# Output projection weights split twice, first gate and up products in another order, and squares of three norms summed on TensorE

## The chip, the cores and the metric

The kernel runs on one core of a Trainium2 chip. A core has a matrix engine (TensorE, PE in the rows; its weight loads are PEld), a vector engine (VectorE, DVE), an engine for functions of one element (ScalarE, ACT), GpSimd (POOL) and a queue that issues transfers (SyncE, SP). Each works its own list of instructions in order; semaphores tie the lists together. The metric is the time of one execution on the device in microseconds, from the first to the last instruction and the little around them.

## The reference

Two decoder layers work on 1024 tokens of width 1024 in f32. Each layer normalises its input, projects it with one matrix for three token mixers, joins their outputs, projects them back (`w_out`) and adds; then it normalises again, and a feed-forward part of width 2816 with gate, up and down follows. A last norm ends it. Cut to what matters:

```python
def rms_norm(x, g):
    y = x * rsqrt(mean(x * x, axis=-1) + 1e-6)
    return y * g

for l in range(2):
    h = rms_norm(x, attn_norm_g[l])
    pa, pb, pc = split(h @ w_in[l])
    ya, yb, yc = rwkv7(pa), dilated_attention(pb), latent_attention(pc)
    x = x + concat(ya, yb, yc) @ w_out[l]
    h = rms_norm(x, ffn_norm_g[l])
    x = x + (silu(h @ w_gate[l]) * (h @ w_up[l])) @ w_down[l]
return rms_norm(x, final_norm_g)
```

## The kernel before

Activations lie transposed: the model's width on the 128 partitions (8 tiles, `KD`), tokens along the columns, in two halves of 512 (`hf`). To reach f32 accuracy a factor is split into a high part, rounded to a faster format (a cast on ScalarE), and a low part, the difference (`split`, on GpSimd or VectorE). `mm3` makes three matmuls from high times high and the two mixed terms. So each weight tile of 128 x 512 costs a load (`wr`), a cast (`wh`), a subtraction (`wl`) and then feeds 4 times 3 matmuls.

The work is written as many small strands (generators). `Flow.run` keeps a clock of estimates for each engine and always lets the strand go on that could start first, so the order of every queue comes out of its costs, and a change in one strand can shift the others. `loader` feeds the weights: `raws` limits the raw tiles, `ring` the split ones that wait. For keys where `again(k)` is true it splits nothing: the first half of the sequence has written the pair of parts to `pairs_dram`, and the second half reads both back. Before, that holds for the input projection ("in") and the output projection ("wo").

In `ffn`, the output projection runs over 8 output tiles for each half (`wo`), adds the residual (`add_x`), and `normed(hf)` normalises that half. Its result is cast and split (`put`), and sums and differences of the halves are formed (`sums`), because gate and up are multiplied by a scheme of seven products for each 2 x 2 block (`PRODUCTS`, `ORDER`). Products 1 and 2 need no sums. Product 2 goes into the bank of product 1 and so waits until ScalarE has copied that out as `u` (`gather`, `f.read[1]`). For the first `EARLY` = 8 blocks, products 1 and 2 are made ahead of everything else, one block after the other.

A norm (`rstds`) squares each of the 8 tiles on ScalarE, adds the squares on VectorE (`acc`, 7 additions) and has TensorE sum that over the partitions: 4 products with one column for 512 tokens, into a small bank `ssum` (`mean_squares`). Then a square root by iteration follows on VectorE (`rsqrt`, tiles `rh`, `ry`, `rt`) and TensorE spreads it by transposes. `norm1(hf)` does it in front of the input projection, and `last_norm` at the end in three parts of 512, 256 and 256 tokens (`PARTS`) while TensorE still works on the last products of the down projection (`dn`).

Of the kernel before, what the change touches and what calls it, by code (L numbers as in the profile page):

```python
# [10 lines left out]
F32 = mybir.dt.float32  # L11
# [7 lines left out]
L = 2  # L19
T = 1024  # L20
D = 1024
HALF = 512
KD = 8
# [7 lines left out]
EARLY = 8  # L31
# [199 lines left out]
def trunk(ctx: ExitStack, tc: tile.TileContext, xT, pos, vec, con, first, w_in, small, uq, uqr, ukv,  # L231
# [3 lines left out]
    F = Flow()  # L235
# [21 lines left out]
    def mm(out, lhsT, rhs, start, stop, again=False):  # L257

        n, m = cols(rhs), cols(lhsT)
        if lhsT.dtype == F32R:  # L260
            F.op("pe", max(n, 2 * m) * 0.4167 + 3)
        else:
            F.op("pe", 4 * max(n, m) * 0.4167 + 6)
        kw = {"skip_group_check": True} if again else {}
        nc.tensor.matmul(out=out, lhsT=lhsT, rhs=rhs, start=start, stop=stop, **kw)  # L265
# [78 lines left out]
    def few_bank(name):  # L344

        yield Need([few])
        t = yield from bank(name)
        owner[id(t)] = (banks, t, few)
        return t
# [12 lines left out]
    def room(level):  # L362

        return lambda: sum(max(n, 0) for lv, n in reserve.items() if lv < level)
# [74 lines left out]
    def vcol(l, name, i=0):  # L439
        o = l * NVEC + VEC[name] + i  # L440
        return vecs[:, o:o + 1]
# [23 lines left out]
    def split(src, hi, lo, eng):  # L465
# [4 lines left out]
        tt(eng, lo, src, f32(hi), ALU.subtract)  # L470

    raws, ring = Slots(NRAW), Slots(NW)
    pairs_dram = {"in": drp.tile([L, 18, 2, 2, 128, HALF], F32, name="pairs_in"),
                  "wo": drp.tile([L, KD, 2, 2, 128, HALF], F32, name="pairs_wo")}
    at_layer = [0]

    def again(k):
        return k[0] in ("in", "wo") and k[2] == 1

    there = {}  # L480

# [170 lines left out]
            stt(y, t, 1.5, y, ALU.add, ALU.mult)  # L652
        return y

    def mean_squares(xs, where, n, keep, w=HALF):

        acc = None
        mean = cons[:, CON["mean"] + MEANS[n]:CON["mean"] + MEANS[n] + 1]
        squares, ahead = events(len(xs)), Slots(3)

        def square():
            for x, ev in zip(xs, squares):
                x = yield x
                yield Need([ahead])
                sq = yield from page(where, "sq", keep=keep)
                yield "act"
                activation(sq[:, :w], x, ACTF.Square)
                F.set(ev, sq)

        F.spawn(square(), 2)  # L670
        for ev in squares:
            sq = yield ev
            if acc is None:
                acc = sq
            else:
                yield "dve"
                tt("dve", acc[:, :w], acc[:, :w], sq[:, :w], ALU.add)
                free(sq)
                F.give(ahead)
        if squared.t is None:  # L680
            F.set(squared, acc)
        s = yield from few_bank("ssum")
        yield "pe"
        for c in range(w // 128):
            mm(s[:, c:c + 1], acc[:, c * 128:(c + 1) * 128], mean, True, True)
        free(acc)
        return s

    def rstds(xs, where, n, keep=0, w=HALF):

        s = yield from mean_squares(xs, where, n, keep, w)
        y = yield from rsqrt(s[:, 0:w // 128], w // 128, 1e-6, ALU.add)
        yield "pe"
        for c in range(w // 128):
            transpose(s[:, c * 128:(c + 1) * 128], y[:, c:c + 1].to_broadcast([128, 128]))
        return s
# [13 lines left out]
            transpose(s[:, cs_], sq[:, cs_])  # L710
        return s

    def norm(xs, g, out, where, tmp, n=D, keep_x=False, keep=0):

        got, k = [None] * len(xs), ["hx", ("hhi", F32R), ("hlo", F32R)]
        if len(xs) < 3:
            t = yield from pages(where, k * len(xs), keep=keep)
            got = [t[3 * i:3 * i + 3] for i in range(len(xs))]
        r = yield from rstds(xs, tmp, n, keep)
        done = []  # L720

        def one(i, r):
            t, hi, lo = got[i] or (yield from pages(where, k, keep=keep))
            yield "dve"
            stt(t, xs[i].val, g(i), r, ALU.mult, ALU.mult)
            if not keep_x:
                free(xs[i].val)
            done.append(i)
            if len(done) == len(xs):
                free(r)  # L730
            yield from split(t, hi, lo, sub_eng())
            free(t)
            F.set(out[i], (hi, lo))

        for i in range(len(xs)):
            F.spawn(one(i, r), 3)
# [230 lines left out]
    def in_items(l):  # L967
# [5 lines left out]
                    out += units(("in", l, hf, 14), w_in[l, 14])  # L973
        return out

    def out_items(l):
        out = [u for hf in range(2) for c in range(KD) for u in units(("wo", l, hf, c), w_out[l, c])]
        def down(st, s):
            n = (st[1] - st[0]) * 128
            per = HALF // n  # L980
            return [(("d", l, s, c0), [w_down[l, c0 + i, :, st[0] * 128:st[1] * 128] for i in range(per)])
                    for c0 in range(0, KD, per)]

        todo = [(m_, n) for n in range(len(PAIRS)) for m_ in "gu"]

        def blocks(w, a, b, c0=0, n=HALF):

            return [[w[i][:, c0 + o:c0 + o + n]] for i, o in ((a, 0), (b, 0), (b, n), (a, n))]

        mats = {"g": w_gate[l], "u": w_up[l]}  # L990
        for m_, n in todo[:EARLY]:
            a = mats[m_][PAIRS[n][0]]
            out += [((m_, l, n, 1), [a[:, 0:HALF]]), ((m_, l, n, 2), [a[:, HALF:]])]
        for i, (m_, n) in enumerate(todo[:-2]):
            rs = ORDER if i >= EARLY else ORDER[1:3] + ORDER[4:]
            out.append((("S", [(m_, l, n)], rs), [blocks(mats[m_], *PAIRS[n])]))
        out.append((("S", [(m_, l, n) for m_, n in todo[-2:]], ORDER), [blocks(mats[m_], *PAIRS[n]) for m_, n in todo[-2:]]))
        for s in range(NS // KS):
            for c in range(0, KD, 4):
                out.append((("S", [("s", l, s, c), ("s", l, s, c + 2)], ORDER),  # L1000
                            [blocks(w_down[l], i, i + 1, s * 256 * KS, 128 * KS) for i in (c, c + 2)]))
        for s, st in enumerate(STAGES):
            out += down(st, s)
        return out

    def layer(l):
# [14 lines left out]
        def norm1(hf):  # L1021
            xs = x_here if l and hf == 0 else events(KD)
            if xs is not x_here:
                for c in range(KD):
                    F.spawn(load_x(xsrc, c, hf, ["gp"], xs[c], xs_done[c][hf] if l else None, room(1)), 2)
            if hf == 0 and l == 0:
                yield from norm_later(xs)
                return
            yield from norm(xs, lambda i: vcol(l, "g1", i), h[hf], ["gp"], ["gp"], keep=room(1))

        rms = Event()

# [1031 lines left out]
        def ffn():  # L2064
# [126 lines left out]
            def product(key, f, r, B, last=False, n=4):  # L2191
                i, first = BANK[r]
                if first:
                    f.bank[i] = yield from bank(f.name)
                else:
                    yield f.read[{2: 1, 4: 7, 3: 5}[r]]
                p = f.bank[i]
                w = yield W[(*key, r)]
                for k in range(n):
                    b = yield B[r][k]  # L2200
                    s = slice(k * 128, k * 128 + 128)
                    yield "pe"
                    mm3(p, (w[0][:, s], w[1][:, s]), b, first and k == 0, k == n - 1, not first)
                    if last:
                        free(*b)
                drop(w)
                F.set(f.done[r])
# [148 lines left out]
            F.give(raws, 4)  # L2356
            todo = [(m_, n) for n in range(len(PAIRS)) for m_ in "gu"]
            fours = {}
            for m_, n in todo[:EARLY]:
                f = fours[m_, n] = Four("gu")  # L2360
                F.spawn(gather(m_, PAIRS[n], f), 2)
                for r in (1, 2):
                    yield from product((m_, l, n), f, r, Bg)
            for i, (m_, n) in enumerate(todo):
                pair = i >= len(todo) - 2
                if i >= EARLY:
# [120 lines left out]
            if l == L - 1:  # L2487
                def last_norm(hf, c0, c1):
                    xs = xf[hf, c0]
                    r = yield from rstds(xs, where, D, w=c1 - c0)  # L2490
                    for c in range(KD):
                        xt, o = xs[c].val, L * NVEC + c
                        yield "dve"
                        stt(xt, xt, vecs[:, o:o + 1], r[:, 0:c1 - c0], ALU.mult, ALU.mult)
                        yield "dma"
                        dma(outT[c, hf, :, c0:c1], xt, 512 * (c1 - c0))
                        if c1 == HALF:
                            free(xd[c][hf].val)
                    free(r)

                for part in PARTS:
                    F.spawn(last_norm(*part), 2)
# [193 lines left out]
```

## Time and profile before

| | |
|---|---|
| median of 3 runs | 2660.67 us (2658.49 to 2663.81) |
| profiled execution | 2660.13 us, span 2658.3 us |
| TensorE busy | 2553.1 us, 96% of the span |
| VectorE, ScalarE, GpSimd busy | 1720.5, 1127.1, 1121.7 us |
| mean granted TensorE clock | 0.975 |

TensorE's share says that nearly everything lies beside its matmuls. The ends of matmuls are modelled, so a busy TensorE is not TensorE at its peak. Short waits and stretches at half clock are what is left around the work.

### The profile page before, as it was taken

What the parts mean: (1) busy time and instruction counts of PE and PEld (TensorE: products, weight loads), DVE (VectorE), ACT (ScalarE), POOL (GpSimd) and SP (SyncE); (2) the same over time, 40 slices, a digit from 0 to 9 for tenths busy, and PEclk for the clock granted to TensorE, in tenths of its full rate; (3) what the DMA queues carried; (4) which work ended last, traced back from release to release, by engine and by line L of the source; (5) the groups of instructions that cost most, each with busy time, mean ns of one, the idle gap of its engine ahead of it and who ended that gap; (6) DMA issues with size and microseconds to landing.
All of it is one profiled execution on the core that took longest, in us unless ns stands there. A gap on an engine that the chain in (4) does not pass through costs nothing. (4 is left out here: it accounts for less than half of the span.)

```text
span 2658.3 us, 38921 instructions
## 1 busy us (share of the span) xinstructions
PE 2553.1 (96%) x13112; PEld 2045.8 (77%) x13112; DVE 1720.5 (65%) x3410; ACT 1127.1 (42%) x2287; POOL 1121.7 (42%) x882
## 2 busy tenths in 40 slices
PE   7899999999999999999999998999998999999998
PEld 5677865787787888888877787658876888888887
DVE  6856567764778666556567365776448876665556
ACT  6433266662434343322354333766534334333221
POOL 3522132353654444465454122314536444444660
PEclk9899979999999999999999999999999999999999
DMA  7563301139335444796476341101681544349861
GB/s 258 186 235 112 107 22 61 39 131 343 131 134 192 150 171 146 252 351 240 151 256 239 114 170 26 56 27 56 224 313 61 191 170 166 134 141 352 285 205 64
DMA packets 249624, 442.73 MB, mean 167 GB/s; under 512 B 29136, under 2 KB 46800, under 8 KB 249296
## 3 DMA queue, kind: packets, MB, share of 16 engines
q1 hardware_dynamic: 249424, 440.24, 48.2%
q8 instruction: 103, 1.69, 0.3%
q14 instruction: 97, 0.79, 0.1%
HBM read 277.99 MB, written 158.47 MB: 164 GB/s over the span
## 5 line engine op out<-in xcount | busy, mean ns | idle before, releaser
L300 POOL TENSOR_TENSOR wl<-wr,wh 128x512 fp32r<-128x512 f32 (+1 forms) x272 | 400.6, 1484 | 397.0 <-ACT wh L294 301.3
L265 PE MATMUL gu<-hhi,wh 128*128 128x512 f32 x1232 | 483.4, 393 | 20.5 <-ACT u L294 13.3
L265 PE MATMUL gu<-hhi,wl 128*128 128x512 f32 x1232 | 480.5, 391 | 1.1 <-POOL wl L300 1.0
L265 PE MATMUL gu<-hlo,wh 128*128 128x512 f32 x1232 | 481.0, 390 | 0.0
L265 PEld LDWEIGHTS gu<-hhi,wh 128*128 128x128 f32 x1232 | 232.2, 188 | 78.6 <-ACT u L294 16.3
L294 ACT CAST wh<-wr 128x512 fp32r<-128x512 f32 (+1 forms) x392 | 226.1, 591 | 107.4 <-POOL wl L300 31.2
L265 PEld LDWEIGHTS gu<-hhi,wl 128*128 128x128 f32 x1232 | 232.3, 189 | 50.9 <-POOL wl L300 2.0
L265 PEld LDWEIGHTS gu<-hlo,wh 128*128 128x128 f32 x1232 | 232.3, 189 | 47.3
L300 POOL TENSOR_TENSOR wl<-s,wh 128x512 fp32r<-128x512 f32 (+1 forms) x136 | 180.3, 1334 | 192.5 <-ACT wh L294 83.0
L265 PE MATMUL dn<-bhi,wh 128*128 128x512 f32 (+1 forms) x664 | 251.7, 380 | 0.7 <-issue 0.7
L265 PE MATMUL dn<-bhi,wl 128*128 128x512 f32 (+1 forms) x664 | 251.5, 379 | 0.0
L265 PE MATMUL dn<-blo,wh 128*128 128x512 f32 (+1 forms) x664 | 251.5, 379 | 0.0
L265 PE MATMUL inp<-hhi,wh 128*128 128x512 f32 x512 | 217.3, 424 | 13.8 <-ACT wh L294 13.8
L294 ACT CAST wh<-s 128x512 fp32r<-128x512 f32 (+1 forms) x204 | 116.6, 581 | 229.9 <-DVE s L300 189.6
L265 PE MATMUL inp<-hhi,wl 128*128 128x512 f32 x512 | 207.6, 406 | 1.3 <-POOL wl L300 1.3
L265 PE MATMUL inp<-hlo,wh 128*128 128x512 f32 x512 | 207.4, 405 | 0.0
L300 DVE TENSOR_TENSOR x<-x,dn 128x512 f32<-128x512 f32 (+1 forms) x160 | 104.4, 657 | 111.5 <-PE dn L265 82.9
L300 DVE TENSOR_TENSOR v<-u,gu 128x512 f32<-128x512 f32 x132 | 90.0, 682 | 129.2 <-PE gu L265 125.7
L300 POOL TENSOR_TENSOR v<-v 128x512 f32<-128x512 f32 x66 | 97.2, 1476 | 135.6 <-DVE v L300 127.2
L300 POOL TENSOR_TENSOR Hd<-H,pc 128x256 f32<-128x256 f32 x32 | 25.4, 793 | 284.0 <-DVE H L300 254.7
L265 PEld LDWEIGHTS dn<-bhi,wh 128*128 128x128 f32 x664 | 124.9, 188 | 25.4 <-issue 1.5
L265 PEld LDWEIGHTS dn<-bhi,wl 128*128 128x128 f32 x664 | 124.9, 188 | 23.4
(319 smaller groups left out, 5500.0 us busy)
## 6 DMA issues: line engine op xcount, KB each, us to landing
act_dram<-ahi SPq DMA_DIRECT2D x142, 256.0 KB
act_dram<-alo SPq DMA_DIRECT2D x142, 256.0 KB
bhi<-act_dram SPq DMA_DIRECT2D x142, 256.0 KB
blo<-act_dram SPq DMA_DIRECT2D x142, 256.0 KB
wr<-in_w_gate_dram SPq DMA_DIRECT2D x104, 256.0 KB
wr<-in_w_up_dram SPq DMA_DIRECT2D x104, 256.0 KB
wr<-in_w_in_dram SPq DMA_DIRECT2D x72, 256.0 KB
pairs_in<-wh SPq DMA_DIRECT2D x72, 256.0 KB
```

The source lines that it names most:

```text
L265: nc.tensor.matmul(out=out, lhsT=lhsT, rhs=rhs, start=start, stop=stop, **kw)
L294: nc.scalar.copy(out=out, in_=in_)
L300: ENG[eng].tensor_tensor(out=out, in0=a, in1=b, op=op)
```

## The change

It has three edits. First, only the input projection's weights are kept as pairs; the output projection's are loaded and split in both halves. Second, the first products of gate and up are issued in another order: product 2 of a block comes after product 1 of the next block. The weights are asked for in the same order. Third, in three norms (the second half in front of the input projection in both layers, counted as `norm1(1)`, and the last norm) TensorE multiplies each square as it comes and adds up in the bank; VectorE adds nothing.

```diff
-    pairs_dram = {"in": drp.tile([L, 18, 2, 2, 128, HALF], F32, name="pairs_in"),
-                  "wo": drp.tile([L, KD, 2, 2, 128, HALF], F32, name="pairs_wo")}
+    pairs_dram = {"in": drp.tile([L, 18, 2, 2, 128, HALF], F32, name="pairs_in")}
...
-        return k[0] in ("in", "wo") and k[2] == 1
+        return k[0] in pairs_dram and k[2] == 1
...
+        if by_pe:
+            s = yield from few_bank("ssum")
+            for i, ev in enumerate(squares):
+                sq = yield ev
+                yield "pe"
+                for c in range(w // 128):
+                    mm(s[:, c:c + 1], sq[:, c * 128:(c + 1) * 128], mean, i + c == 0, i == len(xs) - 1 and c == w // 128 - 1)
+                free(sq)
+                F.give(ahead)
+            return s
...
+    def early(todo):
+
+        two = [[(*t, r) for t in todo[:EARLY]] for r in (1, 2)]
+        out = [two[0][0]]
+        for i in range(EARLY):
+            out += two[0][i + 1:i + 2] + [two[1][i]]
+        return out
...
-        for m_, n in todo[:EARLY]:
-            a = mats[m_][PAIRS[n][0]]
-            out += [((m_, l, n, 1), [a[:, 0:HALF]]), ((m_, l, n, 2), [a[:, HALF:]])]
+        for m_, n, r in early(todo):
+            out.append(((m_, l, n, r), [mats[m_][PAIRS[n][0]][:, (r - 1) * HALF:r * HALF]]))
...
-            yield from norm(xs, lambda i: vcol(l, "g1", i), h[hf], ["gp"], ["gp"], keep=room(1))
+            yield from norm(xs, lambda i: vcol(l, "g1", i), h[hf], ["gp"], ["gp"], keep=room(1), by_pe=hf == 1)
...
-            for m_, n in todo[:EARLY]:
-                f = fours[m_, n] = Four("gu")
-                F.spawn(gather(m_, PAIRS[n], f), 2)
-                for r in (1, 2):
-                    yield from product((m_, l, n), f, r, Bg)
+            for m_, n, r in early(todo):
+                if r == 1:
+                    fours[m_, n] = Four("gu")
+                    F.spawn(gather(m_, PAIRS[n], fours[m_, n]), 2)
+                yield from product((m_, l, n), fours[m_, n], r, Bg)
...
-                    r = yield from rstds(xs, where, D, w=c1 - c0)
+                    r = yield from rstds(xs, where, D, w=c1 - c0, by_pe=True)
```

How the lists move is shown at three places. The queue of transfers (SP) in layer 0, between the two halves of the output projection; `wh` and `wl` are the pair of weight parts, `pj<-mix_dram` are mixers' outputs for the second half, `park_dram` takes the residual. Before:

```order
L328 DMA wh<-pairs_wo 128x512
L328 DMA wl<-pairs_wo 128x512
L328 DMA pj<-mix_dram 128x512 x3
L328 DMA park_dram<-x 128x512 x3
L328 DMA x<-in_xT_dram 128x512
L328 DMA park_dram<-x 128x512 x5
```

Now:

```order
L328 DMA wr<-in_w_out_dram 128x512 x2
L328 DMA x<-in_xT_dram 128x512
L328 DMA pj<-mix_dram 128x512
L328 DMA park_dram<-x 128x512 x2
L328 DMA wr<-in_w_out_dram 128x512
L328 DMA pj<-mix_dram 128x512 x2
L328 DMA wr<-in_w_out_dram 128x512
L328 DMA pj<-mix_dram 128x512 x2
L328 DMA x<-in_xT_dram 128x512
```

The pair reads are gone, raw weights (`wr`) stand between the rest, and the last loads of the mixers' outputs stand ahead of most of the second half's weights instead of behind the first pair reads.

ScalarE in layer 0 during the first products of gate and up: `u<-gu` copies product 1 of a block out of its bank (the copies shown are those of the fourth and fifth block), `hhi<-hx` casts normed rows, `a<-gu` is silu on a finished pair of products. Before:

```order
L290 ACTIVATE a<-gu 128x512
L294 CAST hhi<-hx 128x512 x3
L294 CAST wh<-wr 128x512
L294 COPY u<-gu 128x512
L294 CAST hhi<-hx 128x512 x2
L294 CAST wh<-wr 128x512
L294 CAST hhi<-hx 128x512 x5
L294 COPY u<-gu 128x512
```

Now (the copy shown is the fifth block's):

```order
L290 ACTIVATE a<-gu 128x512
L294 CAST hhi<-hx 128x512 x3
L294 CAST wh<-wr 128x512
L294 COPY u<-gu 128x512
L294 CAST wh<-wr 128x512
L294 CAST hhi<-hx 128x512 x3
L294 CAST wh<-wr 128x512
```

The fifth copy has moved up: from all blocks' first one on, 19 casts of normed rows stood ahead of it, now 12. On TensorE the matmuls between a block's product 1 and its product 2 were 3 to 35 before, where the order also drew parts of later first products forward; now they are one or two whole products, 12 or 24.

TensorE at the very end, last products of the down projection (`dn`, with the numbers of the buffers) and the third part of the last norm. Before:

```order
L265 MATMUL dn_26168<-bhi_25286,wh_25741 128x256
L265 MATMUL dn_26168<-blo_25287,wh_25741 128x256
L265 MATMUL dn_26168<-bhi_25286,wl_25742 128x256
L265 MATMUL dn_26168<-bhi_25507,wh_25741 128x256
L265 MATMUL dn_26168<-blo_25508,wh_25741 128x256
L265 MATMUL dn_26168<-bhi_25507,wl_25742 128x256
L265 MATMUL ssum_26201<-cons_72,sq_26055 128x1 x2
L275 MATMUL ssum_26201<-cons_72,ry_26204 128x128 x2
```

Now:

```order
L265 MATMUL dn_26258<-blo_25296,wh_25784 128x256
L265 MATMUL dn_26258<-bhi_25295,wl_25785 128x256
L265 MATMUL dn_26258<-bhi_25327,wh_25784 128x256
L265 MATMUL dn_26258<-blo_25328,wh_25784 128x256
L265 MATMUL dn_26258<-bhi_25327,wl_25785 128x256
L265 MATMUL ssum_26079<-cons_72,sq_26266 128x1 x2
L265 MATMUL dn_26258<-bhi_25357,wh_25784 128x256
L265 MATMUL dn_26258<-blo_25358,wh_25784 128x256
L265 MATMUL dn_26258<-bhi_25357,wl_25785 128x256
L265 MATMUL ssum_26079<-cons_72,sq_26277 128x1 x2
L275 MATMUL ssum_26079<-cons_72,ry_26281 128x128 x2
```

The sum over all squares was one row (two products, one for each 128 tokens) after the last matmul; now a row for each square stands between the matmuls, and the last one stays behind them. In the two in-projections the new rows stand in the same way between the `inp` products.

## Rows read from the trace of the kernel before

**Rows 1.** Waits of TensorE: who for whom, us in all, times, longest
```profile
PE ssum L265 <- DVE sq L300: 14.5, 6, 5.1
...
PE gu L265 <- ACT u L294: 13.3, 5, 4.4
...
PE ssum L275 <- DVE ry L309: 10.8, 7, 2.5
```

**Rows 2.** Timeline, TensorE, output projection: start, us, what, [idle before]
```profile
635.00 1.02 PE L265 MATMUL ssum<-cons,sq 128*128 128x1 f32 x8 [2.31 <-DVE sq L300]
...
640.46 1.12 PE L275 MATMUL ssum<-cons,ry 128*128 128x128 f32 x4 [2.50 <-DVE ry L309]
...
1939.19 1.05 PE L265 MATMUL ssum<-cons,sq 128*128 128x1 f32 x8 [2.23 <-DVE sq L300]
```

**Rows 3.** Five stretches with a lowered clock; the first line names the columns
```profile
core 0: us, PE busy (x) PEld busy (x) DVE busy (x) ACT busy (x) POOL busy (x), PEclk, DMA share, GB/s
66.00:77.00 11.00, 8.14 (x24) 6.80 (x25) 10.40 (x20) 2.98 (x6) 5.52 (x5) 0.53 0.51 175
636.00:644.00 8.00, 5.50 (x18) 4.02 (x18) 7.08 (x18) 3.07 (x6) 2.82 (x3) 0.57 1.05 404
720.00:729.00 9.00, 5.80 (x15) 4.55 (x16) 8.96 (x8) 3.06 (x6) 9.00 (x6) 0.62 0.25 86
...
1940.00:1945.00 5.00, 5.00 (x19) 3.96 (x19) 2.86 (x14) 0.62 (x1) 0.85 (x1) 0.66 1.05 402
2015.00:2025.00 10.00, 7.55 (x26) 5.94 (x26) 10.00 (x10) 5.56 (x10) 8.01 (x5) 0.83 0.29 91
```

**Rows 4.** Timeline of ScalarE, and a line group of 590:652 (busy, mean ns)
```profile
635.68 1.91 ACT L294 CAST mhi<-pj 128x512 fp32r<-128x512 f32 x3 [1.55 <-DMA pj<-mix_dram]
...
L300 POOL TENSOR_TENSOR wl<-wr,wh 128x512 fp32r<-128x512 f32 x11 | 14.2, 1299 | 14.1 <-ACT wh L294 5.9 <-DMA pj<-mix_dram 5.9 <-issue 2.2
```

**Rows 5.** Timeline, ScalarE and TensorE, early products of layer 0
```profile
722.57 0.58 ACT L294 COPY u<-gu 128x512 f32<-128x512 f32 x1
...
723.20 0.79 PE L265 MATMUL gu<-hhi,wh 128*128 128x512 f32 x1 [4.40 <-ACT u L294]
```

**Rows 6.** Timeline, TensorE: two matmuls of 512 columns in a row
```profile
740.21 0.39 PE L265 MATMUL gu<-hhi,wh 128*128 128x512 f32 x1
740.43 0.39 PE L265 MATMUL gu<-hlo,wh 128*128 128x512 f32 x1
```

**Rows 7.** Timeline, VectorE: sixth product, low weights and first use, layers 0, 1
```profile
732.07 1.77 DVE L300 TENSOR_TENSOR wl<-s,wh 128x512 fp32r<-128x512 f32 x1
...
743.58 0.69 DVE L300 TENSOR_TENSOR u<-u,gu 128x512 f32<-128x512 f32 x1
...
2036.06 1.75 DVE L300 TENSOR_TENSOR wl<-s,wh 128x512 fp32r<-128x512 f32 x1
...
2047.53 0.69 DVE L300 TENSOR_TENSOR u<-u,gu 128x512 f32<-128x512 f32 x1 [0.18 <-PE gu L265]
```

**Rows 8.** Timeline, weight loads of TensorE (PEld) in the last norm
```profile
2623.38 0.98 PEld L265 LDWEIGHTS ssum<-cons,sq 128*128 128x128 f32 x8
2624.29 0.19 PEld L265 LDWEIGHTS dn<-bhi,wh 128*128 128x128 f32 x1
```

**Rows 9.** Timeline, TensorE: longest waits in the two in-projections
```profile
68.86 1.44 PE L265 MATMUL ssum<-cons,sq 128*128 128x1 f32 x6 [5.10 <-DVE sq L300]
...
1404.41 0.90 PE L275 MATMUL hsum<-cons,sq 128*128 128x128 f32 x3 [4.83 <-DVE sq L313]
```

**Rows 10.** Line group of VectorE from 56 to 69 us
```profile
L300 DVE TENSOR_TENSOR sq<-sq 128x512 f32<-128x512 f32 x7 | 7.6, 1079 | 2.6 <-ACT sq L290 2.6
```

**Rows 11.** The last stage before the end, as one stretch; columns as rows 3
```profile
2600.00:2645.00 45.00, 45.00 (x297) 41.45 (x296) 29.41 (x79) 11.54 (x24) 1.29 (x1) 1.00 0.14 50
```

**Rows 12.** Timeline, VectorE and TensorE: the chain after the last product
```profile
2647.39 0.41 DVE L300 TENSOR_TENSOR sq<-sq 128x256 f32<-128x256 f32 x1
...
2647.95 0.58 PE L265 MATMUL ssum<-cons,sq 128*128 128x1 f32 x4 [2.18 <-DVE sq L300]
```

More of the change, by code (lines that the diff above doesn't have):

```diff
@@ L653, in rsqrt, with mean_squares @@
         return y
-    def mean_squares(xs, where, n, keep, w=HALF):
+    def mean_squares(xs, where, n, keep, w=HALF, by_pe=False):
         acc = None
@@ L687, in mean_squares, with rstds @@
         return s
-    def rstds(xs, where, n, keep=0, w=HALF):
-        s = yield from mean_squares(xs, where, n, keep, w)
+    def rstds(xs, where, n, keep=0, w=HALF, by_pe=False):
+        s = yield from mean_squares(xs, where, n, keep, w, by_pe)
         y = yield from rsqrt(s[:, 0:w // 128], w // 128, 1e-6, ALU.add)
@@ L711, in head_rsqrt, with norm @@
         return s
-    def norm(xs, g, out, where, tmp, n=D, keep_x=False, keep=0):
+    def norm(xs, g, out, where, tmp, n=D, keep_x=False, keep=0, by_pe=False):
         got, k = [None] * len(xs), ["hx", ("hhi", F32R), ("hlo", F32R)]
@@ L718, in norm @@
             got = [t[3 * i:3 * i + 3] for i in range(len(xs))]
-        r = yield from rstds(xs, tmp, n, keep)
+        r = yield from rstds(xs, tmp, n, keep, by_pe=by_pe)
         done = []
```

## Prediction

> **What bounds the kernel now.** I read the waits of TensorE first, then its timeline around the longest of them, then the granted clock beside each, and last the other engines in the same microseconds. The reader is to see that TensorE works nearly all the time, so that added matmuls cost their time in full and only its few waits can be won back. Three of the largest of these waits belong to this change [rows 1]: 14.5 us before the column sums of a norm (ssum), 13.3 us before gate and up's first products, 10.8 us before the transposes that spread a norm's result. Each long wait also lowers the granted clock for some microseconds, to 0.5, which is 1.2 GHz instead of 2.4 [rows 3]. The loss to that is worked out as busy time times what is missing of the clock.
>
> All sums are made against the profiled execution, 2660.13 us (span 2658.3). The median of the three runs is 0.5 us above it.
>
> **Output projection's weights.** At the end of the first half of the sequence, layer 0, TensorE waits 2.31 us for the last square and 2.50 us for the square root; in layer 1 it waits 2.23 us for the square [rows 2]. The clock then costs 5.50 x 0.43 = 2.4 and 5.00 x 0.34 = 1.7 us [rows 3]. That is 11.1 us in all. Why does it have nothing else to do? The second half's matmuls need the mixers' outputs, and the first of these is cast at 635.68, when its load lands [rows 4]. The queue order shows why it is late: the last three of these loads stand behind pair writes and pair reads. The DMA share is then 1.05 [rows 3], so the transfers are the limit. The change takes away, in each layer, 32 writes and 32 reads of 256 KB and adds 16 reads: 12 MB less. The mixers' outputs now stand in the queue before the second half's weights, and 18 matmuls stand between the squares and the transposes instead of 5. So the gap should be filled. The 32 added splits take 1.30 us each on GpSimd [rows 4] and a cast on ScalarE, one for every 12 matmuls; 12 x 0.22 = 2.6 us of TensorE's work covers one [rows 6]. If that cover were gone for the first of a half, a load, cast and subtraction would cost about 2 us. Ends: -11.1 and +2. I take -9, near the measured waits, since the mechanism is seen whole and only some of the wait for the square root may stay.
>
> **First products of gate and up.** The waits of 13.3 us [rows 1] and the clock, 5.80 x 0.38 = 2.2 and 7.55 x 0.17 = 1.3 us [rows 3], make 16.8 us. The longest wait, 4.40 us, ends when ScalarE has copied u out of the bank [rows 5]. The copy is not slow (0.58 us); it stands behind the casts of the normed rows, which wait for VectorE. In the new order this copy, the fifth, stands behind 12 of these casts instead of 19. But VectorE's own order is nearly unchanged, and the next kind of product (the sixth) needs weights whose low part VectorE ends at 732.07 + 1.77 = 733.84 and at 2036.06 + 1.75 = 2037.81 [rows 7]. Its result is added to u at 743.58 and 2047.53 [rows 7]; less the product's own 2.7 us, it could have been issued without a break from 740.9 and 2044.8. So 7 us in each layer can be won before TensorE stands there instead, 14 in all. Ends: 0 (the wait only moves, and costs the clock there) and -16.8. I take -9, two thirds of what VectorE allows, because a shorter wait at the new place also costs some clock.
>
> **Squares added up by TensorE: the price.** A norm over 8 tiles has 8 groups of four products with one column instead of 1, so 28 more products. In the trace the 8 weight loads of one such group (two for each product in f32) begin at 2623.38 and the next matmul's load at 2624.29 [rows 8]: 0.91 us for a group of four. The columns cost nothing; the loads do. Seven more groups are 6.4 us per norm of 512 columns.
>
> The Trainium skill, TensorE: Matmul & The Clock Gate, section "Step-by-step: what each phase is for", says that TensorE pulls weight loads ahead of the matmuls in flight, so that the next tile's weights load while this one is multiplied. By that rule the groups would be nearly free. Rows 8 show it for the first load of a group at most: the other seven have only one-column products to hide behind.
>
> **The two norms of the in-projection (second half, layers 0 and 1).** In layer 0 TensorE waits 5.10 us for the sum [rows 9], and the clock costs 8.14 x 0.47 = 3.8 us [rows 3]: 8.9 us. VectorE spends 7.6 us on the seven additions there [rows 10], in a stretch where it hardly rests, because GpSimd's work makes each 1.08 us long. These go. TensorE gets 6.4 us of groups, spread between products of the projection, so it fills its wait instead of standing. Balance -2.5, and VectorE's later waiters come some 1.5 us sooner: -4. Ends: +6.4 (nothing returns) and -10. In layer 1 the wait is 4.83 us, for another chain that VectorE delivers late [rows 9]; the additions removed are worth about as much as the groups cost. I take 0, ends +6.4 and -6.
>
> **The last norm.** Here TensorE works 45.00 of 45.00 us at full clock up to the end of the last product [rows 11], so the groups are paid in full. The tokens are normed in three parts: 512, 256 and 256 columns. The first adds seven groups of four (6.4 us), the second seven groups of two (3.2), and of the third's eight groups seven stand before the last matmul of the down projection (3.2, where there was none): 12.8 us. After it, TensorE waits 2.18 us for the last addition [rows 12]; that addition (0.41 us) and one in front of it leave the chain, with their handovers: -1.0. Together +11.8, ends +10 and +13.
>
> **Sum.** -9 - 9 - 4 + 0 + 11.8 = -10.2, and 2660.13 - 10.2 = 2649.9; I say 2650.
>
> **Rivals.**
> A: the weights' two stages give everything back: -11.1 - 16.8 - 4 + 0 + 11.8 = -20, so 2640. For it: the mixers' loads clearly move up, and the output projection's earlier end lets VectorE begin sooner. Against: VectorE is without rest in the early products (8.96 of 9 us [rows 3]).
> B: the wait in the early products only moves to the sixth product's weights: gate and up give 2 instead of 9, the rest as forecast, 2657, no change that can be told. For it: rows 7 and VectorE's unchanged order. Against: 7 us per layer lie between VectorE's end and TensorE's start.
> C, slower: the groups are paid everywhere. In the in-projections they come on top, because what TensorE waits for is other work of VectorE and not the seven additions; then both norms cost 6.4, and -9 - 9 + 12.8 + 11.8 = +6.6, 2667. It decides the sign as soon as the stalls return less than the 24.6 us that all groups cost. For it: the 4.83 us of layer 1 are not a wait for these sums. Against: layer 0's 5.10 us are.
> D: the loads are hidden. The norms then give -8.9 and -4.8, the last one -1.0, and the sum is -32.7, 2627. Rows 8 speak against it. This is the skill's rule above.
>
> **How the numbers follow.** Forecast 0.44 (its own range 2643 to 2656), A 0.22, B 0.17, C 0.13, D 0.04. About 0.2%, 5.3 us, can be told from no change. Faster: 0.39 of the forecast's, 0.21 of A's, 0.05 of B's and D's 0.04, 0.69. Same: 0.05, 0.01, 0.11 and 0.02 of C's, 0.19. Slower: 0.12. The order of all five queues is replanned by the change, which can move any other wait by a few us; the forecast's own range has that in it. The range from 2636 to 2664 leaves out D, most of C and a fifth of A.
>
> **What would show it right or wrong.** Right: no wait of TensorE above 1 us among the output projection's matmuls and full clock there; the waits for ScalarE's u below 5 us in total; 0.9 us between the matmuls on both sides of each new group; the last matmul of the down projection coming 12 to 13 us later after the stage's first one than now. A step is wrong if the mixers' second half is still cast after TensorE has run dry, if the groups cost under 0.3 us, if a wait for a square (ScalarE) shows in front of them, or if the sixth product's weights become the early products' wait of more than 4 us. The whole is wrong if the stages that the change does not name move by more than 5 us together.

## The result, and the profile after

The changed kernel is slower: 2673.3 to 2680.9 us in three runs against 2658.5 to 2663.8 us in four, ratio 1.0059 (95% interval 1.0041 to 1.0077), so about +15.7 us. Measured once more beside 19 runs of the kernel before, the ratio was 1.0055 (1.0033 to 1.0076). The first profiled execution took 3050.5 us at a mean granted clock of 0.775 and is left out of these figures, so the profile shown here comes from the second measurement (2686.1 us, span 2684.0, clock 0.968). It is 10 us above the median of its own runs (2675.9), which matters for layer 1 below.

The stages tell where the time is. A stage runs from its first matmul on TensorE to the first one of the next stage (the last one to its own last matmul), in us; "mixers" is what lies between the input projection's last matmul and the output projection's first.

| stage | before | after | difference |
|---|---|---|---|
| input projection, layer 0 | 334.4 | 345.4 | +11.0 |
| mixers, layer 0 | 239.3 | 234.7 | -4.6 |
| output projection, layer 0 | 102.0 | 94.1 | -7.9 |
| gate and up, layer 0 | 437.0 | 438.4 | +1.4 |
| down, layer 0 | 206.9 | 206.1 | -0.8 |
| input projection, layer 1 | 315.8 | 330.8 | +15.0 |
| mixers, layer 1 | 246.9 | 250.7 | +3.9 |
| output projection, layer 1 | 96.3 | 90.5 | -5.8 |
| gate and up, layer 1 | 439.3 | 441.1 | +1.8 |
| down with the last norm, layer 1 | 219.0 | 231.6 | +12.6 |
| after the last product | 12.6 | 11.9 | -0.7 |

TensorE's waits after, as in [rows 1] (who for whom, us in all, times, longest):

```profile
PE gu L265 <- ACT u L294: 14.6, 4, 6.0
...
PE ssum L275 <- DVE ry L309: 10.0, 5, 3.5
...
PE ssum L265 <- ACT sq L290: 2.1, 2, 1.1
PE ssum L265 <- DVE sq L300: 1.5, 1, 1.5
```

The waits for sums of squares fell from 14.5 to 3.6 us, as they were meant to. The waits for `u` did not fall: 14.6 us instead of 13.3, in fewer and longer pieces.

The output projection before, as one stretch for each layer (columns as in [rows 3]):

```profile
582.70:684.80 102.10, 97.29 (x435) 79.88 (x434) 39.96 (x65) 33.19 (x60) 36.66 (x28) 0.97 0.87 310
1891.20:1987.70 96.50, 93.24 (x407) 76.08 (x406) 35.44 (x59) 28.59 (x50) 35.06 (x26) 0.98 0.90 318
```

And after:

```profile
588.90:683.10 94.20, 94.20 (x429) 78.07 (x428) 44.88 (x65) 39.90 (x72) 57.77 (x44) 1.00 0.60 205
1909.00:1999.70 90.70, 90.70 (x407) 75.23 (x406) 39.78 (x59) 37.02 (x66) 55.48 (x42) 1.00 0.61 207
```

TensorE now works without idle time and at full clock there, and the DMA share is down from 0.87 to 0.60. GpSimd works some 20 us more in each layer (36.66 to 57.77, 35.06 to 55.48) and nobody waits for it.

In layer 0's in-projection the 31 us around the norm read so before:

```profile
54.00:85.00 31.00, 23.44 (x106) 18.29 (x107) 27.61 (x43) 14.78 (x28) 16.25 (x13) 0.78 0.49 170
```

And after:

```profile
54.00:85.00 31.00, 29.73 (x118) 25.93 (x119) 15.29 (x27) 10.94 (x22) 14.76 (x12) 0.50 0.51 178
```

TensorE is busy for 29.73 us instead of 23.44, VectorE for 15.29 instead of 27.61. Both are what the change wanted. But the granted clock is 0.50 over the whole stretch, where it was 0.78. The timeline of TensorE after shows what stands there, in place of the 5.10 us of waiting in [rows 9]:

```profile
55.27 0.80 PE L265 MATMUL inp<-hhi,wh 128*128 128x512 f32 x1 [3.21 <-ACT wh L294]
55.85 1.81 PE L265 MATMUL ssum<-cons,sq 128*128 128x1 f32 x8
57.53 0.77 PE L265 MATMUL inp<-hlo,wh 128*128 128x512 f32 x1
58.10 0.63 PE L265 MATMUL inp<-hhi,wl 128*128 128x512 f32 x1
58.53 1.70 PE L265 MATMUL ssum<-cons,sq 128*128 128x1 f32 x8
```

A group of four (8 records, two for each product in f32) takes 1.70 us, nearly twice the 0.91 us of [rows 8].

### The profile page after: what moved, and what is told of

Same layout as the page of the kernel before. It is cut to its first block, busy times and chain, and to the rows that moved or that the text cites. A ratio compares the mean times of both kernels' runs of the same rounds, so it can differ in the third digit from the quotient of the medians.

```text
span 3048.4 us, 39261 instructions
## 1 busy us (share of the span) xinstructions
PE 3001.7 (98%) x13336; PEld 2206.2 (72%) x13336; DVE 1705.3 (56%) x3376; ACT 1141.3 (37%) x2314; POOL 1118.9 (37%) x914
## 5 line engine op out<-in xcount | busy, mean ns | idle before, releaser
L265 PE MATMUL gu<-hhi,wh 128*128 128x512 f32 x1232 | 539.2, 438 | 6.2 <-ACT u L294 6.2
L265 PE MATMUL gu<-hhi,wl 128*128 128x512 f32 x1232 | 539.7, 438 | 0.0
L265 PE MATMUL gu<-hlo,wh 128*128 128x512 f32 x1232 | 537.5, 436 | 0.0
L265 PE MATMUL dn<-bhi,wh 128*128 128x512 f32 (+1 forms) x664 | 283.6, 427 | 0.0
L265 PE MATMUL dn<-blo,wh 128*128 128x512 f32 (+1 forms) x664 | 281.1, 423 | 0.0
L265 PE MATMUL dn<-bhi,wl 128*128 128x512 f32 (+1 forms) x664 | 281.1, 424 | 0.0
L265 PE MATMUL inp<-hhi,wh 128*128 128x512 f32 x512 | 247.9, 484 | 11.9 <-ACT wh L294 11.9
L265 PE MATMUL inp<-hhi,wl 128*128 128x512 f32 x512 | 241.6, 472 | 0.4 <-POOL wl L300 0.3
L265 PE MATMUL inp<-hlo,wh 128*128 128x512 f32 x512 | 239.4, 468 | 0.0
L265 PEld LDWEIGHTS dn<-blo,wh 128*128 128x128 f32 x664 | 130.5, 197 | 43.3
```

## Experiments

Each kernel was measured beside the kernel before; every time is a ratio to those runs of before, with its 95% interval, and the difference is that ratio in us of 2663.

**The changed kernel once more.** No edit.

> The changed kernel once more, unaltered, for a profile at full clock. Its time was 1.0059 of the time before, +15.7 us. Theory 1 (all groups of one-column products are paid in full, 24.6 us, and the two weights' stages return some 9): no TensorE wait above 1 us among the output projection's matmuls, 0.9 us for each added group, and the stages that the change does not name agree with before within 5 us. Theory 2 (the new order of the queues costs time elsewhere): a stage that the change does not name, the mixers between the input projection's end and the output projection's start above all (239 us in layer 0, 247 us in layer 1 before), is longer by 10 us or more.

The result is the profile above. The mixers are 4.6 us shorter in layer 0 and 3.9 us longer in layer 1, 0.7 us together, so the new order of the queues is not where the time went: theory 2 falls. Theory 1 holds for the output projection's waits and the last norm, but the 11.0 and 15.0 us of the two input projections are more than the 6.4 us that it gives each, and a group in layer 0 takes 1.70 us.

**The last norm alone.** Before, with one line changed:

```diff
-                    r = yield from rstds(xs, where, D, w=c1 - c0)
+                    r = yield from rstds(xs, where, D, w=c1 - c0, by_pe=True)
```

> The kernel before with the squares of the last norm alone summed by TensorE. The order of TensorE's list differs only in the last stage. The prediction's term: +11.8 us, ends +10 and +13, and the last matmul of the down projection 12.8 us later after the stage's first. If weight loads hide behind the matmuls in flight: -1 us. If a group costs more than the row of before shows (a change from the projection's products to one-column products and back that the row leaves out): over +14 us.

Measured: 1.0047 (1.0028 to 1.0066), +12.5 us. The stage was 13.4 us longer (219.0 to 232.4), the end behind it 1.1 us shorter. The sums' own instructions in one stretch of before (all that name `ssum`; columns as in [rows 3], without GpSimd's):

```profile
2620.00:2655.00 35.00, 3.70 (x24) 3.02 (x24) 13.08 (x27) 0.00 (x0) 0.93 0.30 106
```

And here:

```profile
2620.00:2664.00 44.00, 12.49 (x96) 12.26 (x96) 9.54 (x19) 0.00 (x0) 1.00 0.20 72
```

TensorE's share grows by 8.8 us for 72 more records (two for each product in f32) in this stretch alone, 0.122 us for each. They are paid one by one, with the clock at 1.00. The Trainium skill, TensorE: Matmul & The Clock Gate, section "Step-by-step: what each phase is for", has the next tile's weights loading while this one is multiplied; by these rows next to nothing is hidden where the product behind the load has a single column.

**The two in-projection norms alone, and each by itself.**

```diff
-            yield from norm(xs, lambda i: vcol(l, "g1", i), h[hf], ["gp"], ["gp"], keep=room(1))
+            yield from norm(xs, lambda i: vcol(l, "g1", i), h[hf], ["gp"], ["gp"], keep=room(1), by_pe=hf == 1)
```

and for one layer alone `by_pe=hf == 1 and l == 0`, or `l == 1`.

> The kernel before with the squares of the two in-projection norms alone summed by TensorE. The prediction's terms: -4 in layer 0 and 0 in layer 1, -4 us together. Theory 1, groups paid in full there too: +12.8 us, since what TensorE waits for is other work than the seven additions. Theory 2, the new order costs in other stages: the in-projection itself is shorter or equal and the mixers behind it are longer.

> The kernel before with the squares of layer 0's in-projection norm alone summed by TensorE. The prediction's term: -4 us. Theory of the clock (one-column products between wide ones keep the granted clock at 0.50, which had recovered there before): +5 to +9 us, a stretch of some 30 us at 0.50 from about 54 us on, and the mixers behind it some us shorter since VectorE is relieved. Theory of the bare price, full clock: +6.4 us in the in-projection, no longer stretch at 0.50.

> The kernel before with the squares of layer 1's in-projection norm alone summed by TensorE. The prediction's term: 0, ends +6.4 and -6. From the run with both norms less the run with layer 0's alone: 0. If the price of seven groups is paid in full there: +6.4 us.

Measured: both 1.0040 (1.0024 to 1.0056), +10.7 us; layer 0 alone 1.0040 (1.0026 to 1.0055), +10.7 us; layer 1 alone 1.0013 (0.9997 to 1.0029), +3.5 us, not told from nothing. So the loss is in layer 0, with its middle above the 5 to 9 us of the clock's theory (6.9 to 14.6 in the interval) and beyond the upper end of my range, +6.4. In the profile with layer 0 alone the input projection is 10.6 us longer and the mixers behind it 5.6 us shorter. The stretch of 31 us:

```profile
54.00:85.00 31.00, 29.96 (x120) 26.11 (x121) 15.51 (x28) 10.96 (x21) 14.80 (x12) 0.51 0.51 178
```

The same picture as in the changed kernel, with no other part of the change present. It repeats: in this stretch the clock is 0.50 or 0.51 in this trace and those of the changed kernel and of both norms, and 0.78 to 0.83 in all ten traces that leave layer 0's norm as it was before.

**Fewer one-column products, and wide ones between them.** Both have layer 0's norm alone. The first kernel adds the squares two by two on VectorE and so makes four groups instead of eight:

```diff
+                if i % 2 == 0:
+                    sq2 = yield ev
+                    continue
                 sq = yield ev
+                yield "dve"
+                tt("dve", sq[:, :w], sq2[:, :w], sq[:, :w], ALU.add)
...
```

> Layer 0's in-projection norm alone, with VectorE adding the squares two by two (four additions) and TensorE summing four groups instead of eight: three groups more than before, 2.7 us. Theory of the clock (one-column products between wide ones keep it at 0.50): with half of them the stretch at 0.50 from about 54 us on is clearly shorter than the 30.7 us of eight groups, and the kernel is 0 to +5 us against before. If that long stretch comes from the three microseconds of waiting for the first weights and not from the groups: again about 30 us, and +6 to +9 us.

The second keeps the eight groups and puts a wide product behind each of the first seven:

```diff
                     mm(s[:, c:c + 1], sq[:, c * 128:(c + 1) * 128], mean, i + c == 0, ...)
+                if i < len(xs) - 1:
+                    mm(s[:, 128:512], sq[:, 0:128], sq[:, 128:512], False, False)
...
```

> As the run with layer 0's in-projection norm alone, and after each of the first seven groups one more f32 product of 384 columns into unused columns of the same bank, overwritten later: 7 x 4 x 384 columns, 4.5 us of added work at full clock and 9 us at half. Theory of the clock (it stays low because the one-column products leave the array nearly empty): the stretch at 0.50 gets shorter than 25 us and the added work is mostly given back, the time within 3 us of the run without it. If the clock stays low for another reason: the stretch lasts 35 to 40 us and the run is 7 to 9 us slower than the one without it.

The same 31 us with four groups:

```profile
54.00:85.00 31.00, 28.45 (x137) 24.03 (x138) 26.41 (x44) 14.65 (x29) 18.64 (x15) 0.73 0.55 189
```

With eight groups and wide products behind them:

```profile
54.00:85.00 31.00, 28.64 (x138) 23.35 (x139) 13.18 (x39) 12.53 (x22) 15.50 (x13) 0.72 0.60 204
```

Time at half clock in the stretch is (1 - clock) x 31 / 0.5: 13.6 us before, 30.4 with eight groups, 16.7 with four, 17.4 with eight and wide products between them. So it is the one-column products that keep the clock down here, not the wait ahead of them: that was 3.56 us before, 3.21 with eight groups, and 5.46 in the run with four, the longest. With the wide products the input projection became 4.3 us shorter (344.9 to 340.6), although by the count of columns in the expectation it does 4.5 us more work at full clock.

The whole time did not follow: 1.0060 (1.0038 to 1.0082), +16.0 us, against +10.7 without them, where I had expected them within 3 us of each other. The intervals overlap, and in the profile the rest is 7.9 us longer; I can't tell whether by the order of the mixers, which the added work shifts too, or by chance. Four groups cost 1.0021 (1.0008 to 1.0035), +5.6 us, between the two ranges expected and about half of eight, though these intervals overlap too. The two profiled executions are equally long (span 2666.7 us): with four groups the clock fell again later (0.51 from 306 to 320 us). By the same reckoning over the whole input projection it was at half for some 51 us with four groups, 44 with eight, and 31 before and with the wide products; the stage with four took 343.4 us, only 1.5 less than with eight. So the runs show what keeps the clock down in the stretch; what that costs the whole time they do not settle.

**The weights' two edits, together and apart.** Together is the changed kernel without `by_pe`. The output projection alone is before with `again` as in the change and without

```diff
-                  "wo": drp.tile([L, KD, 2, 2, 128, HALF], F32, name="pairs_wo")}
```

and the order alone is before with `early` as in the change.

> Both weights' edits (the output projection's weights split in both halves, products 1 and 2 of gate and up in the new order), no sums by TensorE. The prediction's terms: -18 us. Theory 1 (groups paid in full, 24.6 us of the +15.7): -9 us. Theory 2 (the loss comes from the new order of the queues that these two edits bring): 0 to +8 us, with the loss in the mixers.

> The kernel before with the output projection's weights alone split in both halves. The prediction's term: -9 us, ends -11.1 and +2. If the two weights' edits add up as the run with both showed (its output projections were 7.9 and 5.8 us shorter on TensorE, gate and up 2.8 longer and 0.6 shorter): -10 to -14 us, more than the 11.1 us of waits and clock that I had counted. If the output projection gains only together with the new order of gate and up: -5 us or less.

> The kernel before with the new order of gate and up's first products alone. The prediction's term: -9 us, ends 0 and -16.8. Rival B (the wait only moves, since VectorE delivers the summed weights of the sixth product no earlier): -2 to +3 us, and one wait of about 6 us for ScalarE's u in each layer in place of the three of 1 to 4.4 us, behind a cast of summed weights that waits for VectorE.

Measured: together 0.9955 (0.9938 to 0.9972), -12.0 us; the output projection alone 0.9945 (0.9930 to 0.9961), -14.6 us; the order alone 1.0009 (0.9997 to 1.0021), +2.4 us, not told from nothing. Rival B holds for gate and up. TensorE with the order alone, layer 0, against [rows 5]:

```profile
713.77 0.50 PE L265 MATMUL gu<-hhi,wh 128*128 128x512 f32 x1 [1.26 <-ACT u L294]
...
730.91 0.79 PE L265 MATMUL gu<-hhi,wh 128*128 128x512 f32 x1 [5.96 <-ACT u L294]
```

What ends the long wait stands in the changed kernel's lists. VectorE:

```profile
728.77 1.74 DVE L300 TENSOR_TENSOR s<-wr 128x512 f32<-128x512 f32 x1
730.44 1.74 DVE L300 TENSOR_TENSOR hlo<-hx,hhi 128x512 fp32r<-128x512 f32 x1
732.11 0.68 DVE L300 TENSOR_TENSOR s<-s,wr 128x512 f32<-128x512 f32 x1
...
733.47 0.69 DVE L300 TENSOR_TENSOR wl<-s,wh 128x512 fp32r<-128x512 f32 x1
```

ScalarE and TensorE behind it:

```profile
732.82 0.62 ACT L294 CAST wh<-s 128x512 fp32r<-128x512 f32 x1 [5.01 <-DVE s L300]
733.34 0.58 ACT L294 COPY u<-gu 128x512 f32<-128x512 f32 x1
...
733.98 0.79 PE L265 MATMUL gu<-hhi,wh 128*128 128x512 f32 x1 [5.96 <-ACT u L294]
```

This copy is the seventh block's; it stands on ScalarE behind the first cast of the sixth product's summed weights (`s`), and that waits 5.01 us for VectorE, which takes 1.74 us for a sum and for a low part while GpSimd works beside it (up to 731.6), and 0.68 us for the next sum. The name in the wait is ScalarE's; the late engine is VectorE. So the wait did not move to the sixth product itself, as rival B has it, but it ends with that product's weights all the same, by way of ScalarE's queue. With the order alone it is there in both layers, 5.96 and 5.93 us.

**More blocks in front.** `EARLY` set to 10 with both edits, to 10 with the old order, to 12 with the old order (the last two with the output projection's edit).

> Both weights' edits, no sums by TensorE, and ten blocks instead of eight whose products 1 and 2 come first. Theory (TensorE waits 5.96 us in each layer because VectorE brings the summed weights of the sixth product late): the two blocks more are 48 matmuls of 0.225 us, 10.8 us of work in front of that wait in each layer, so it shrinks below 2 us and the kernel is 6 to 10 us faster than the run with eight blocks (2649.1), 2639 to 2643. Rival (the two blocks' own splits and copies delay the summed weights as long): the wait stays above 4 us, 2647 to 2652.

> The output projection's weights split in both halves, the old order of the first products, ten blocks instead of eight. In the old order TensorE waits at product 2 of the blocks in the middle, not at the end, so more blocks behind do not help: 2644 to 2648, as with eight (2645.6). If all these waits go back to VectorE's lateness in the sums: 4 to 8 us faster.

> As the run with the output projection's weights and ten blocks in the old order, with twelve. Theory that the waits come from blocks in the middle: 2644 to 2649, no gain over ten. Theory of VectorE's lateness in the sums: 2 us or more below ten blocks.

Measured: 0.9940 (0.9919 to 0.9960), -16.0 us; 0.9950 (0.9931 to 0.9970), -13.3 us; 1.0044 (1.0029 to 1.0059), +11.7 us. Ten blocks with the new order, TensorE's waits in gate and up:

```profile
PE gu L265 <- ACT ahi L294: 9.1, 6, 2.7
PE gu L265 <- DVE v L300: 7.3, 14, 1.7
PE gu L265 <- ACT u L294: 5.9, 4, 2.3
```

With eight blocks and the same two edits these were 2.2, 4.1 and 14.5 us. The wait of 5.96 us is gone, as the theory said, and what is left for `u` stands at earlier copies (2.3 us at most). But the two waits for the steps behind it grew from 2.2 and 4.1 us to 9.1 and 7.3, by as much, and the time (2646.9) is at the rival's lower edge and not in the theory's 2639 to 2643: the gain over eight blocks (-16.0 against -12.0) can't be told from chance. Ten blocks in the old order made no difference, as expected. With twelve, a wait for casts of weights comes up, of which before has 0.4 us, and the wait for `v` grows from 3.2:

```profile
PE gu L265 <- ACT wh L294: 11.8, 4, 3.3
PE gu L265 <- ACT u L294: 8.8, 2, 4.4
PE gu L265 <- DVE v L300: 7.8, 13, 1.8
```

My expectation of no difference there was a miss: gate and up took 451 and 452 us instead of 437 and 438 with eight blocks.

**The changed kernel without layer 0's norm.**

```diff
-... keep=room(1), by_pe=hf == 1)
+... keep=room(1), by_pe=hf == 1 and l == 1)
```

> The changed kernel with the in-projection norm of layer 0 summed by VectorE as before, the other three parts kept. If the parts add up (weights -12.0, last norm +12.5, layer 0 +10.7, layer 1 about 0): 10.7 us faster than the changed kernel, about 2664, no change from before. If the missing time of the prediction lies in the whole plan and not in layer 0's norm: still 2670 or more.

Measured: 1.0005 (0.9993 to 1.0016), 2663.7 us, as the parts add up. Without this one norm the kernel is not slower than before. By the sum of the parts the same would hold without the last norm, which was not run.

The output projection's edit by itself (2645.6 us) and both edits with ten blocks (2646.9 us) can't be told apart; both beat the kernel before and the changed one, and the first is the smaller change.

## Why the prediction was wrong

Sum of my terms: -10.2. Measured one by one: -12.0 for the weights, +10.7 for the in-projections, +12.5 for the last norm, +11.2 together, against +14.6 and +15.7 for the whole. Two steps failed, the second and the third below.

- **Output projection, -9 predicted, -14.6 measured.** Right in mechanism, too small, and outside my end of -11.1, though the interval (-18.6 to -10.4) reaches it. TensorE's idle time there was 102.10 - 97.29 + 96.50 - 93.24 = 8.1 us, and I had counted 7.0, without the short waits; the clock cost 0.03 x 102.1 + 0.02 x 96.5 = 5 us and not 4.1. All of it came back (the two stages were 13.7 us shorter), and I had taken two off.
- **First products of gate and up, -9 predicted, +2.4 (-0.8 to +5.6) measured.** The step that failed is "So 7 us in each layer can be won before TensorE stands there instead". I took the time at which the sixth product's weights were used before (740.9) as the time at which they were needed. It was late because TensorE had waited before it. With those waits gone TensorE is at the last early product but one at 728.0 (733.98 less 5.96), 45.1 us after the stage's first matmul at 682.9. The low part of the summed weights comes no earlier than before: 733.84 less 684.7 is 49.1 us [rows 7], 733.47 plus its 0.69 less 682.9 is 51.3 now. Rival B had the limit, and I gave it 0.17.
- **Layer 0's in-projection, -4 predicted, +10.7 (6.9 to 14.6) measured.** The step that failed is "so it fills its wait instead of standing". It does fill it: the 5.10 us are gone, and no wait stands between the groups. But I priced the groups at full clock and counted on getting back what the clock had cost. [Rows 9] held a group at half clock, 1.44 us for six records or 0.24 each; I went by the 0.11 of [rows 8]. The whole stage of before, and with layer 0's norm alone:

```profile
8.97:343.36 334.39, 314.48 (x2004) 247.40 (x2004) 216.95 (x469) 142.18 (x261) 107.22 (x96) 0.95 0.51 173
8.70:353.65 344.95, 327.94 (x2082) 261.38 (x2082) 211.82 (x465) 141.99 (x263) 106.98 (x98) 0.94 0.49 168
```

  TensorE's busy time grew by 13.5 us, its idle time fell by only 2.9 (19.9 to 17.0), because other waits grew. The 13.5 are nearly the groups' 6.4 and at most 6.9 for 44 instead of 31 us at half clock. Of the 5.6 us that the mixers then took less, part is work that now stands in the in-projection: 78 records of TensorE more there and 22 fewer in the mixers. How the +10.7 of the whole time divides between price and clock stays open within its interval.
- **Layer 1's in-projection, 0 predicted, +3.5 (-0.8 to +7.7) measured.** Not wrong within what can be told; the clock makes it uneven (below).
- **Last norm, +11.8 predicted, +12.5 measured; 12.3 in the profile.** Right: TensorE had no idle time there, and each added record was paid.
- **The stages "that the change does not name"** moved by -0.7 us (mixers, -4.6 and +3.9) and -0.8 us (down, layer 0). That caveat was not what happened.

With only layer 0's in-projection put at its measured value the sum would be -10.2 + 14.7 = +4.5, with only gate and up's +1.2; it takes both to make the kernel clearly slower, and the output projection's better result makes up for part of them. Rival C had the sign, with +6.6, but not for its reason: the wait of layer 0 was for these sums and did vanish. What came in its place was the price of the groups and the clock. D falls with the last norm.

## What to carry to other kernels

Work that fills a wait of TensorE isn't free because the wait was there: many one-column products between wide ones can leave the clock at half (here 0.50 with TensorE busy for 29.73 of 31.00 us), which the busy share doesn't show, so read the granted clock of the stretch beside it. When several waits stand one behind the other, work out when the later input is needed once the earlier waits are gone, not when it was used before. Where TensorE has no idle time, as in the last stage here, each added product is paid in full, so leave such sums to an engine with time to spare.

## What the runs showed of the hardware that was not expected

The granted clock fell while TensorE had no idle time at all. In layer 1 of the changed kernel the groups run from 1369.8 to 1391.7; two stretches of it:

```profile
1372.00:1378.00 6.00, 6.00 (x42) 5.43 (x42) 1.89 (x5) 4.94 (x10) 3.06 (x3) 1.00 0.62 225
1378.00:1396.00 18.00, 18.00 (x80) 15.78 (x79) 6.11 (x31) 1.46 (x3) 2.69 (x3) 0.53 0.19 68
```

TensorE's list in this stage is the same, matmul for matmul, in the run with the two in-projection norms alone; there the groups run from 1380.6 to 1396.4:

```profile
1378.00:1384.00 6.00, 6.00 (x38) 5.26 (x37) 3.96 (x9) 4.26 (x8) 1.72 (x2) 1.00 0.94 312
1384.00:1396.00 12.00, 12.00 (x98) 10.84 (x97) 4.00 (x8) 3.92 (x8) 5.74 (x5) 1.00 0.55 193
```

In one execution the clock went to half, in the other it held; the input projection took 330.8 us in the first and 315.9 in the second. Two more traces have the same list in this stage. With layer 1's norm alone the groups ran at 1.00; in the changed kernel without layer 0's norm the clock fell for part of them, again without idle time:

```profile
1366.80:1386.20 19.40, 19.40 (x127) 17.78 (x126) 7.19 (x17) 6.87 (x13) 5.75 (x5) 0.82 0.47 173
```

Why it falls in one and holds in another is open. The twelve times with layer 1's norm alone lie in two bands, five from 2654.0 to 2664.7 at a mean clock of 0.973 to 0.976 and seven from 2668.1 to 2674.4 at 0.968 to 0.973. That these are the two cases is not shown: only one of the twelve (2660.5 us) has a trace. The Trainium skill, TensorE: Matmul & The Clock Gate, section "What's actually happening", says that the clock follows how busy the array has been. The rows here show that a TensorE which the profile calls busy for 18.00 of 18.00 us can be granted 0.53 of it.
